# Index scores rectified in PSUM, half of the u projection dealt out between them, a fourth search tile on VectorE

## The chip, the cores and the metric

The kernel runs on one core of one Trainium2 chip. The metric is the device time of one execution, in microseconds; lower is better. TensorE multiplies into PSUM, VectorE (DVE) and ScalarE (ACT) read and write PSUM and SBUF, GpSimd (POOL) works on SBUF alone, and SyncE (SP) issues most of the DMAs. Each engine works through its own queue in order.

## What is computed

One layer of a hybrid decoder, for 1024 tokens of width 1024, in float32. The part that the change touches:

```python
h = rms_norm(x, norm1_g) * (1.0 + sc1) + sh1
proj = h @ w_in
u_ssm, q, k, v, q_idx, k_idx, w_idx = split(proj)
# S5 head group: diagonal state-space model of u_ssm
# sparse attention head group, per query t:
logits = relu(einsum('bthd,bsd->bths', q_idx, k_idx))          # 8 index heads of 64
score = einsum('bth,bths->bts', w_idx, logits) * IDX_SCALE
score = where(causal, score, -inf)
_, sel = top_k(score, 256)                                     # then attention over the selected keys
```

After that come group norms, one output projection and a squared-ReLU MLP; the change leaves them as they are.

## The kernel before

The 1024 queries are eight tiles of 128. Tiles 0 and 1 have at most 256 causal keys and need no selection; tiles 2 to 7 are the six search tiles, whose score rows are 384, 512, 640, 768, 896 and 1024 wide (`W` in `select`; search tile i is query tile i+2). Float32 products are made of three matmuls on split operands (`mm3`, L90 to L92: high·high, high·low, low·high), so every weight is loaded (`raw`), its high part taken by ScalarE (`wh`, L470) and its low part by GpSimd (`wl`, L472). There are two `raw` buffers and six of `wh` and `wl` each; a group of 256 columns of w_in takes four of the six, a group of 128 columns (the index queries) two.

The parts run as Python generators that `weave` advances by turns. What they issue goes to a scheduler which orders each engine's queue by priority (the order of issue) and by its own estimate of when operands are ready, so a later part can be placed ahead of an earlier one that waits. `later` issues a generator at a lower priority, and `tc.issue_after(ins)` puts the TensorE instructions of its block behind the one named in TensorE's queue.

The stages around the change, with the names of the code:

- `s5_setup` (VectorE, small operations) ends while the index stage has begun. `s5_tables` builds, for each of eight blocks, three tables on GpSimd (12 instructions a block) and stores each to HBM from SP's queue; the S5 scan loads them again much later (`s5_load_tables`, `s5_load_rot`).
- `index_proj`: for four groups of two index heads, `index_q` projects and splits the index queries and `index_score` makes the scores. For each search tile and head it makes two halves of the row in a two-bank PSUM tile (L551, L552), ScalarE writes relu(scale·score) for the whole row into an SBUF tile `r` (L556), and VectorE adds sign·r to the sum in SBUF (L558 for the first head, L560 for the seven others). After the eighth head L517 masks the diagonal block of each tile. The tables are advanced one step each round.
- `proj_qu`: u in two groups of 256 columns, eight tiles each, stored to HBM (L576, L577) and read back in another layout (L579); then q in two groups, with its norm's sums (L592, L593) and `rsqrt_q`.
- `select`: mean and variance of each search tile (L681 to L704), nine threshold passes over all six tiles (L707 to L724; `SEL_DVE` = 0, 1, 5 on VectorE, `SEL_ACT` = 4, 3, 2 on ScalarE), an exact end for each tile on VectorE (L734 to L741), a flag that says whether any row failed (a matmul with ones, L752, then L754, read into a VectorE register for a branch over the exact fallback), and then per tile the bias step that turns scores into 0 or -1e30 (L785 to L790).
- `attention` and `s5` are woven, then `glu`, `ada_rest`, the output projection and the MLP.

## Time and profile before

| | us |
|---|---|
| three runs, median (lowest to highest) | 1360.86 (1357.33 to 1362.24) |
| the profiled execution, its own time | 1360.31 |
| its span in the trace | 1358.5 |
| TensorE busy in the span | 1216.1 (90%) |
| VectorE busy | 1017.4 (75%) |
| ScalarE busy | 616.7 (45%) |
| GpSimd busy | 364.7 (27%) |

The span is the time from the first to the last instruction in the trace; 1.8 us of the execution's own time lie around it. The busy shares are averages over stages that have different limits, so the stage that is changed is read for itself. Matmuls overlap in their pipeline: a TensorE that is shown as wholly busy need not be at its peak, and the distance between the starts of two matmuls tells what one costs.

### The profile page before, as it was taken

The page shows a single profiled execution, that of the slowest core. Times are in us where ns is not written, and L with a number is a line of the kernel's source. Part 1 is how long each engine was busy: PE and PEld are TensorE (multiplying, and loading weights), DVE is VectorE, ACT ScalarE, POOL GpSimd, SP SyncE. Part 2 cuts the span into 40 slices and gives each one's busy share as a digit, 9 for nine tenths or more (in the row PEclk, how much of TensorE's full clock was granted, in tenths as well). Part 3 has the DMA queues.
Part 4 walks back from the last instruction along what each step waited for, and adds up shares of the span by engine and source line. Part 5 has one row for each costly group of instructions (what it writes and reads, how often), then busy time and mean ns, then how long its engine had stood idle before and what let it go on. Part 6 is the DMA issues. An engine that isn't in the chain of part 4 may idle for free.

```text
span 1358.5 us, 18554 instructions
## 1 busy us (share of the span) xinstructions
PE 1216.1 (90%) x6414; PEld 1038.1 (76%) x6414; DVE 1017.4 (75%) x1894; ACT 616.7 (45%) x1231; POOL 364.7 (27%) x350
## 2 busy tenths in 40 slices
PE   4987987935898999999979999999988999999997
PEld 4876887934788889888857788888866878788785
DVE  6599947897978763347795677677678888876887
ACT  6454453584777775724242333333224334333330
POOL 3072799861643453711100000000000000000125
PEclk9797989975899997999989999999998999999999
DMA  9511122350231572422412444433457735436252
GB/s 330 131 41 40 60 97 91 133 149 9 71 103 51 179 231 71 133 78 93 160 66 93 148 146 163 155 141 138 163 197 275 254 95 193 132 95 210 84 185 109
DMA packets 119327, 179.83 MB, mean 132 GB/s; under 512 B 28864, under 2 KB 63680, under 8 KB 119232
## 3 DMA queue, kind: packets, MB, share of 16 engines
q1 hardware_dynamic: 118160, 178.61, 40.1%
q8 instruction: 50, 0.82, 0.3%
q14 instruction: 45, 0.37, 0.1%
q10 hardware_dynamic: 1072, 0.03, 0.0%
HBM read 128.92 MB, written 48.50 MB: 131 GB/s over the span
## 4 chain that ended last, share of the span: by engine, by line
PE 51%; DVE 12%; DMA 4%; ACT 2%; issue 2%; POOL 2%; SPq 1%; DVEq 0%; ACTq 0%; POOLq 0%
PE pS L90 10%; PE pS L91 10%; PE pS L92 10%; PE pg L90 5%; PE pg L91 5%; PE pg L92 5%; DMA awa<-w_ada 2%; PE po L1274 2%; DVE fm L472 2%; PE pg L269 1%; PE pg L1258 1%; DVE acc L1871 1%; DVE acc L1845 1%; DVE fw L472 1%; POOL wol L472 1%
## 5 line engine op out<-in xcount | busy, mean ns | idle before, releaser
L1845 POOL TENSOR_TENSOR acc<-acc,g 128x512 f32<-128x512 f32 x4 | 5.9, 1499 | 579.1 <-DVE acc L1871 579.1
L91 PE MATMUL pg<-wl,hh 128*128 128x256 f32 (+1 forms) x288 | 81.6, 284 | 13.0 <-POOL wl L472 13.0
L470 ACT ACTIVATE fm<-ar 128x512 fp32r<-128x512 f32 x56 | 34.9, 624 | 119.9 <-PE pg L91 55.1
L90 PE MATMUL pg<-wh,hh 128*128 128x256 f32 (+1 forms) x288 | 81.0, 285 | 3.7 <-ACT wh L470 2.6
L1274 PEld LDWEIGHTS po<-v,pt 128*128 128x128 f32 x576 | 77.5, 208 | 6.0 <-ACT pt L1261 3.8
L1274 PE MATMUL po<-v,pt 128*128 128x64 f32 x576 | 78.8, 285 | 3.5 <-ACT pt L1261 3.3
L92 PE MATMUL pg<-wh,hl 128*128 128x256 f32 (+1 forms) x288 | 81.4, 284 | 0.0
L560 DVE SCALAR_TENSOR_TENSOR sc<-r,wsgn,sc 128x384 f32<-128x384 f32 (+5 forms) x42 | 56.0, 1344 | 28.5 <-ACT r L556 27.3
L90 PE MATMUL pS<-fm 128*128 128x512 f32 x160 | 62.2, 400 | 4.7 <-DVE z L1874 4.4
L91 PEld LDWEIGHTS pg<-wl,hh 128*128 128x128 f32 x288 | 55.1, 191 | 14.0 <-POOL wl L472 13.4
L91 PE MATMUL pS<-fm 128*128 128x512 f32 x160 | 63.1, 397 | 0.3 <-DVE fm L472 0.3
L92 PE MATMUL pS<-fm 128*128 128x512 f32 x160 | 62.9, 395 | 0.0
L1245 DVE CUSTOM_DVE_ANT_0 P<-pS,sc,rq 128x384 f32<-128x384 f32 (+5 forms) x48 | 43.9, 941 | 20.9 <-PE pS L1241 12.8
L90 PEld LDWEIGHTS pg<-wh,hh 128*128 128x128 f32 x288 | 54.3, 190 | 5.0 <-ACT wh L470 2.8
L556 ACT ACTIVATE r<-pS,wabs 128x384 f32<-128x384 f32 (+5 forms) x48 | 40.6, 848 | 36.4 <-PE pS L552 27.7
L92 PEld LDWEIGHTS pg<-wh,hl 128*128 128x128 f32 x288 | 54.9, 191 | 0.4
L470 ACT ACTIVATE fw<-ax 128x512 fp32r<-128x512 f32 x42 | 26.2, 623 | 61.1 <-PE pS L91 29.6
L1261 ACT ACTIVATE pt<-pg 128x512 f32<-128x512 f32 (+1 forms) x80 | 42.2, 547 | 22.2 <-PE pg L1258 21.8
L1258 PE MATMUL pg<-ident,P 128*128 128x128 f32 x288 | 49.2, 292 | 3.0 <-DVE zl L1340 1.3
L1247 ACT ACTIVATE P<-P,mx 128x128 f32<-128x128 f32 (+7 forms) x64 | 49.1, 769 | 5.7 <-DVE mx L1245 5.5
L90 PE MATMUL pS<-woh,mh 128*128 128x512 f32 x128 | 51.2, 400 | 0.0
L92 PE MATMUL pS<-woh,ml 128*128 128x512 f32 x128 | 50.9, 398 | 0.0
(606 smaller groups left out, 4154.1 us busy)
## 6 DMA issues: line engine op xcount, KB each, us to landing
awa<-w_ada SPq DMA_DIRECT2D x32, 512.0 KB, 4.3
a_d<-ws SPq DMA_DIRECT2D x64, 256.0 KB, 2.7
wr<-w_ff SPq DMA_DIRECT2D x32, 512.0 KB, 6.3
w1r<-w_ff SPq DMA_DIRECT2D x15, 1024.0 KB, 5.2
ax<-a_d SPq DMA_DIRECT2D x56, 256.0 KB, 2.8
ar<-a_d SPq DMA_DIRECT2D x56, 256.0 KB, 2.9
a_d<-c SPq DMA_DIRECT2D x45, 256.0 KB, 2.0
x<-x SPq DMA_DIRECT2D x16, 512.0 KB, 5.1
```

The source lines that it names most:

```text
L90: T.matmul(out, lh, rh, start=start, stop=False, **kw)
L91: T.matmul(out, lh, rl, start=False, stop=False, **kw)
L92: self.pe = T.matmul(out, ll, rh, start=False, stop=stop, **kw).ins
L470: nc.scalar.activation(hi, x, AF.Copy)
L472: e.tensor_tensor(lo, x, f(hi), op=OP.subtract)
L556: S.activation(rv, ps[:, :, :n], AF.Relu, scale=self.wabs[:, qt, h:h + 1])
L560: V.scalar_tensor_tensor(sc, rv, self.wsgn[:, qt, h:h + 1], sc, op0=OP.mult, op1=OP.add)
L1245: V.tensor_tensor_reduce(pv, ps[:, :nj, :m], bv, scale=self.rq[:, qt, h:h + 1], scalar=-NEG, op0=OP.add, op1=OP.min, accum_out=mx)
L1247: S.activation(p[:, :w], p[:, :w], AF.Exp, scale=-1.0, bias=mx, accum_out=LS[qt][:, h:h + 1])
L1258: T.transpose(ps[:, o:o + 128], P[n][h][:, (k0 + i) * 128:(k0 + i + 1) * 128], self.ident)
L1261: S.activation(pt[:, :m], ps[:, :m], AF.Copy)
L1274: T.matmul(po[:, o:o + HD], pt[:, (2 * i + h) * 128:(2 * i + h + 1) * 128], self.v[:, k0 + i, kv * HD:(kv + 1) * HD], start=(o == 0 and k0 ...
```

## The change

1. Scores. ScalarE's relu writes back into the PSUM tile it reads, half by half, and VectorE adds from PSUM. Rows of 384 and 512 take one bank of the four-buffer ring and one instruction of each; the four wider ones take two halves. The causal mask goes into the first head's pass for the last 128 columns, and L517 goes. The SBUF tiles `r` go (`knd` gets its own two).
2. u. The first group (`proj_u(0)`) is a generator of the index stage, one k-step (three matmuls) per round, and every u matmul is put behind the latest score matmul that has been issued. The second group is issued after the last score and is therefore behind all scores.
3. Tables. Of the eight blocks, the first four are issued in the index stage. Blocks 4 to 7 begin with a small copy on GpSimd that reads `self.gate`, so they wait: for `gs`, which the statistics of `select` make, or, for those issued after the flag, for `need`.
4. Search. Tile 2 (640 wide) moves from ScalarE to VectorE, and VectorE updates the threshold of each tile by two operations on one column instead of three on all of VectorE's columns (two before the loop).
5. Flag. A DMA turns `bad` into a row of one partition and a maximum makes the flag; the matmul goes.
6. Bias steps. They are advanced one for one with the first attention steps, with the S5 steps behind, where before they were issued ahead of both.

```diff
-SEL_DVE = (0, 1, 5)
-SEL_ACT = (4, 3, 2)
+SEL_DVE = (0, 1, 2, 5)
+SEL_ACT = (4, 3)
@@ build
-            self.index_proj(ix, tab)
+            self.index_proj(ix, itertools.islice(tab, 10 * TABG))      # TABG = 4
...
-            for i in range(2 * NT * 2):
+            for i in range(3 * NT):
                 next(qu)
-                next(tab, None)
-                if i % 2 or i >= 29:
+                if self.gate is not None and i < 21:
+                    next(tab, None)
+                if (i + 1) * 17 // (3 * NT) > i * 17 // (3 * NT):
                     self.weave([(sel, 1)], n=1)
             self.weave([(sel, 1)])
-            self.weave([(sel, 1)])
+            next(sel)
             self.weave([(tab, 1)])
...
-            self.weave([(s5, 1)], att, 2, n=2)
+            self.weave([(att, 1), (sel, 1)], s5, 1, until=sel)
             self.weave([(s5, 1)], att, 1)
@@ index_proj
+        u0 = self.proj_u(0)
         for c in range(4):
...
+            gens.append((itertools.islice(u0, 12 if c < 3 else 24), 1 if c < 3 else 2))
             self.weave(gens, tab, TABN)
-        for qt in range(2, 8):
-            dg = self.bias[qt][:, qt * 128:]
-            V.scalar_tensor_tensor(dg, dg, NEG, self.caus, op0=OP.max, op1=OP.min)
+        self.weave([(u0, 1)])
@@ index_score
+                    o = ps[:, j, :n]
+                    ks = slice(j * n, (j + 1) * n)
+                    T.matmul(o, lq, self.kih[:, ks], start=True, stop=False)
+                    self.last_sc = T.matmul(o, lq, self.kil[:, ks], start=False, stop=True).ins
+                    S.activation(o, o, AF.Relu, scale=self.wabs[:, qt, h:h + 1])
+                    sc, sg = self.bias[qt][:, ks], self.wsgn[:, qt, h:h + 1]
+                    if h:
+                        V.scalar_tensor_tensor(sc, o, sg, sc, op0=OP.mult, op1=OP.add)
+                        continue
+                    d = n - 128 if j == nj - 1 else n
+                    V.tensor_scalar(sc[:, :d], o[:, :d], sg, None, op0=OP.mult)
+                    if d < n:
+                        V.scalar_tensor_tensor(sc[:, d:], o[:, d:], sg, self.caus, op0=OP.mult, op1=OP.add)
@@ proj_u (new; proj_qu calls it for the second group)
+        wg = self.load_w([(C_U + c * 256, 256)], 256)
+        yield
+        for t in range(NT):
+            ps = self.bank()
+            tl = slice(t * 128, t * 128 + 128)
+            for k in range(KC):
+                wh, wl = wg[k]
+                with self.tc.issue_after(self.last_sc):
+                    self.mm3(ps[:, :256], self.hh[:, k, tl], self.hl[:, k, tl], wh, wl, k == 0, k == KC - 1)
+                if c == 0:
+                    yield
...
@@ select, in each of the eight passes
-            V.tensor_tensor(d, v[:, :NV], st1[:, k, :NV], op=OP.subtract)
-            V.scalar_tensor_tensor(t[:, :NV], c[:, :NV], float(TOPK), st2[:, k, :NV], op0=OP.is_ge, op1=OP.mult)
-            V.tensor_tensor(v[:, :NV], d, t[:, :NV], op=OP.add)
+                V.tensor_scalar(col(t, i), col(c, i), float(TOPK), st2[:, k, i:i + 1], op0=OP.is_ge, op1=OP.mult)
+                V.tensor_scalar(col(v, i), col(v, i), st1[:, k, i:i + 1], col(t, i), op0=OP.subtract, op1=OP.add)
@@ the flag
-        ps = self.bank()
-        T.matmul(ps[0:1, 0:1], bad, self.ones[:, 0:1], start=True, stop=True)
+        row = sp.tile([1, 128], F32, name="row")
+        nc.sync.dma_start(row, bad)
         fi = sp.tile([1, 1], I32, name="fi")
-        V.tensor_copy(fi, ps[0:1, 0:1])
+        V.tensor_reduce(fi, row, axis=AX.X, op=OP.max)
@@ s5_tables
+            if b >= TABG:
+                G.tensor_copy(cx[:, 0, 0:6], self.gate)
```

## Rows read from the trace of the kernel before

**Rows 1.** The page's first line.

```profile
span 1358.5 us, 18554 instructions
```

**Rows 2.** The table by stage: busy time, instructions, granted clock (PEclk).

```profile
core 0: us, PE busy (x) PEld busy (x) DVE busy (x) ACT busy (x) POOL busy (x), PEclk, DMA share, GB/s
...
174.00:206.00 32.00, 26.11 (x192) 25.32 (x191) 16.10 (x14) 14.72 (x24) 32.00 (x27) 0.89 0.31 101
206.00:242.00 36.00, 28.88 (x215) 27.99 (x214) 24.71 (x20) 13.60 (x21) 36.00 (x30) 0.91 0.29 93
242.00:257.00 15.00, 15.00 (x130) 15.00 (x129) 14.04 (x34) 2.75 (x7) 14.06 (x17) 1.00 0.61 204
257.00:297.00 40.00, 25.23 (x208) 24.41 (x207) 39.34 (x114) 39.59 (x116) 29.80 (x39) 0.91 0.31 94
297.00:318.00 21.00, 0.00 (x0) 0.02 (x1) 20.91 (x82) 3.06 (x10) 3.65 (x9) 0.50 0.34 97
...
330.00:460.00 130.00, 117.12 (x869) 106.85 (x869) 106.00 (x229) 100.85 (x218) 55.55 (x58) 0.94 0.28 78
```

**Rows 3.** TensorE's timeline, 194 to 240 us: start, duration, [idle before <- who ended it].

```profile
194.92 0.58 PE L91 MATMUL pg<-wl,hh 128*128 128x256 f32 x1 [5.89 <-POOL wl L472]
...
235.62 0.58 PE L91 MATMUL pg<-wl,hh 128*128 128x256 f32 x1 [7.12 <-POOL wl L472]
...
239.29 0.28 PE L92 MATMUL pg<-wh,hl 128*128 128x256 f32 x1
239.40 0.28 PE L90 MATMUL pg<-wh,hh 128*128 128x256 f32 x1
```

**Rows 4.** The timeline of GpSimd around 194 and 260 us.

```profile
193.61 2.49 POOL L472 TENSOR_TENSOR wl<-raw,wh 128x512 fp32r<-128x512 f32 x2
...
260.30 1.28 POOL L1046 TENSOR_TENSOR mt<-mt,mx 128x512 f32<-128x512 f32 x1
```

**Rows 5.** Groups by line and shape, VectorE, 100 to 260 us: busy, mean, idle.

```profile
L560 DVE SCALAR_TENSOR_TENSOR sc<-r,wsgn,sc 128x1024 f32<-128x1024 f32 x7 | 11.9, 1700 | 10.8 <-ACT r L556 10.6
...
L560 DVE SCALAR_TENSOR_TENSOR sc<-r,wsgn,sc 128x384 f32<-128x384 f32 x7 | 6.5, 924 | 0.2
```

**Rows 6.** The same view, ScalarE, 100 to 260 us.

```profile
L556 ACT ACTIVATE r<-pS,wabs 128x1024 f32<-128x1024 f32 x8 | 8.9, 1115 | 4.4 <-PE pS L552 4.4
...
L556 ACT ACTIVATE r<-pS,wabs 128x384 f32<-128x384 f32 x8 | 4.6, 581 | 4.3 <-PE pS L552 4.2
```

**Rows 7.** The same view, VectorE, 242 to 323 us.

```profile
L724 DVE TENSOR_TENSOR v<-d,t 128x3 f32<-128x3 f32 x8 | 3.8, 472 | 0.2
...
L738 DVE TENSOR_SCALAR ix<-cx 128x1 f32<-128x1 f32 x6 | 0.9, 149 | 0.0
```

**Rows 8.** The timeline of VectorE, single instructions of scoring, search and flag.

```profile
126.03 0.73 DVE L560 SCALAR_TENSOR_TENSOR sc<-r,wsgn,sc 128x512 f32<-128x512 f32 x1
...
260.21 0.16 DVE L712 SCALAR_TENSOR_TENSOR t<-c,gs 128x3 f32<-128x3 f32 x1
260.41 1.20 DVE L713 TENSOR_TENSOR v<-v,t 128x3 f32<-128x3 f32 x1
...
314.22 0.86 DVE L734 TENSOR_SCALAR_CACHE_REDUCE jv<-sc,hi 128x640 bf16<-128x640 f32 x1
...
318.23 0.15 DVE L754 CAST fi<-pg 1x1 int32<-1x1 f32 x1
...
322.13 0.19 DVE L620 TENSOR_SCALAR rq<-ry 128x48 f32<-128x48 f32 x1 [3.57 <-DVEq L759]
```

**Rows 9.** One line's view, L1159: min, median and max ns, first and last start.

```profile
L1159 DVE SCALAR_TENSOR_TENSOR y<-y,pg x8: 659/680/686, 364.5 to 443.3; 128x512 f32<-128x512 f32 x8
```

**Rows 10.** The timeline of TensorE at the flag.

```profile
318.01 0.19 PE L752 MATMUL pg<-ones,bad 128*1 128x1 f32 x2 [32.09 <-DVE rw L617]
```

**Rows 11.** One line's view, L577: issue to landing of a small store.

```profile
DMA to landing us min/median/max: 1.7/2.0/3.0
```

**Rows 12.** The timeline of SP's queue, the seventh load of an S5 table.

```profile
394.21 0.54 SPq L1074 DMA_DIRECT2D cl<-cl_d  x1
```

More of the change, by code (lines that the diff above doesn't have):

```diff
@@ L1 @@
+import itertools
 from contextlib import ExitStack
@@ L47 @@
 EARLY = 500
-LATER, TABN = 500, 1
+LATER, TABN, TABG = 500, 1, 4
 ON_V = [(k, 0) for k in (1, 2, 3, 5, 6)]
@@ L133, in build @@
             self.select_consts()
-            self.index_proj(ix, tab)
+            self.gate = None
+            self.u_d = self.dram.tile([L, DS], F32, name="u_d")
+            self.index_proj(ix, itertools.islice(tab, 10 * TABG))
             ix_close()
@@ L137, in build @@
             self.u = up.tile([128, 8, DS], F32, name="u")
-            self.u_d = self.dram.tile([L, DS], F32, name="u_d")
             qp, qp_close = self.pool("q", side="left")
@@ L440, in k_norm @@
         self.rstd(rk, self.kss[:, 4 * hf:4 * hf + 4].rearrange("p t h -> p (t h)"), HD, ix)
-        knd = ix.tile([128, NKV, 4, 2, HD], F32, name="knd", tag="r", bufs=3)
+        knd = ix.tile([128, NKV, 4, 2, HD], F32, name="knd", bufs=2)
         yield
@@ L543, in index_score @@
         for qt in range(2, 8):
-            n = (qt + 1) * 64
+            w = (qt + 1) * 128
+            nj = 1 if w <= 512 else 2
+            n = w // nj
             for i in range(2):
                 h = 2 * c + i
-                ps = self.bank2()
+                ps = self.bank()[:, None, :] if nj == 1 else self.bank2()
                 lq = qs[c][i][:, (qt - 2) * 128:(qt - 1) * 128]
-                for j in range(2):
+                for j in range(nj):
                     o = ps[:, j, :n]
-                    T.matmul(o, lq, self.kih[:, j * n:(j + 1) * n], start=True, stop=False)
-                    T.matmul(o, lq, self.kil[:, j * n:(j + 1) * n], start=False, stop=True)
-                sc = self.bias[qt].rearrange("p (j n) -> p j n", j=2)
-                r = ix.tile([128, L], F32, name="r", tag="r", bufs=3)
-                rv = r[:, :2 * n].rearrange("p (j n) -> p j n", j=2)
-                S.activation(rv, ps[:, :, :n], AF.Relu, scale=self.wabs[:, qt, h:h + 1])
-                if h == 0:
-                    V.tensor_scalar(sc, rv, self.wsgn[:, qt, h:h + 1], None, op0=OP.mult)
-                else:
-                    V.scalar_tensor_tensor(sc, rv, self.wsgn[:, qt, h:h + 1], sc, op0=OP.mult, op1=OP.add)
@@ new lines, in index_score, with proj_u @@
+                    d = n - 128 if j == nj - 1 else n
[3 more added lines that the diff above has]
+                yield
+    def proj_u(self, c):
+        nc = self.nc
+        wg = self.load_w([(C_U + c * 256, 256)], 256)
[8 more added lines that the diff above has]
+                if c == 0:
+                    yield
+            us = self.wp.tile([128, 256], F32, name="us", bufs=2)
+            nc.scalar.activation(us, ps[:, :256], AF.Copy)
+            nc.sync.dma_start(self.u_d[tl, c * 256:c * 256 + 256], us)
+            if c:
@@ L565, in proj_qu @@
         V, S, G, T = nc.vector, nc.scalar, nc.gpsimd, nc.tensor
+        u1 = self.proj_u(1)
+        next(u1)
         for c in range(2):
-            wg = self.load_w([(C_U + c * 256, 256)], 256)
             cs = slice(c * 256, c * 256 + 256)
-            for t in range(NT):
-                ps = self.bank()
-                tl = slice(t * 128, t * 128 + 128)
-                for k in range(KC):
-                    wh, wl = wg[k]
-                    self.mm3(ps[:, :256], self.hh[:, k, tl], self.hl[:, k, tl], wh, wl, k == 0, k == KC - 1)
-                us = self.wp.tile([128, 256], F32, name="us", bufs=2)
-                S.activation(us, ps[:, :256], AF.Copy)
-                nc.sync.dma_start(self.u_d[tl, cs], us)
-                yield
+            if c:
+                yield from u1
             nc.sync.dma_start(self.u[:, :, cs], self.u_d[:, cs].rearrange("(m j) n -> m j n", j=8))
@@ L700, in select @@
         V.tensor_tensor(gs, sd, self.slope, op=OP.mult)
+        self.gate = gs
         st1, st2 = (sp.tile([128, K, 6], F32, name=n) for n in ("st1", "st2"))
@@ L711, in select @@
             V.tensor_scalar(jv[:, :W[i]], B[i], col(v, i), None, op0=OP.is_ge, op1=OP.add, accum_out=col(c, i))
-        V.scalar_tensor_tensor(t[:, :NV], c[:, :NV], TOPK - 0.5, gs[:, :NV], op0=OP.subtract, op1=OP.mult)
-        V.tensor_tensor(v[:, :NV], v[:, :NV], t[:, :NV], op=OP.add)
+            V.tensor_scalar(col(t, i), col(c, i), TOPK - 0.5, col(gs, i), op0=OP.subtract, op1=OP.mult)
+            V.tensor_scalar(col(v, i), col(v, i), col(t, i), None, op0=OP.add)
         yield
@@ L750, in select @@
         yield "flag"
-        ps = self.bank()
-        T.matmul(ps[0:1, 0:1], bad, self.ones[:, 0:1], start=True, stop=True)
+        row = sp.tile([1, 128], F32, name="row")
+        nc.sync.dma_start(row, bad)
         fi = sp.tile([1, 1], I32, name="fi")
-        V.tensor_copy(fi, ps[0:1, 0:1])
+        V.tensor_reduce(fi, row, axis=AX.X, op=OP.max)
         X = st(6, "X", I32)
@@ L776, in select @@
             V.tensor_scalar(need, cx, -1.0, float(TOPK), op0=OP.mult, op1=OP.add)
+        self.gate = need
         yield
```

5 lines of the change are left out of this document (2 added, 3 removed).

## The prediction

> **What bounds the kernel now.** I read the table by stage first, because the shares of the whole span hide it, then the timelines of the engines that stand still in a stage, and last single operations for their prices. The edits lie in the stages from about 113 us (first scores) to 330 us (first attention steps); what comes behind has no edge to the wall clock, so I take it that it moves with them as a whole.
>
> From 146 to 242 us the index stage is TensorE's: VectorE is busy for only 16 of the 32 us from 174 to 206 [rows 2]. [...] In this stage the scheduler has put the whole u projection, though u is issued later. Twice TensorE stands still, 5.89 and 7.12 us, for `wl`, the low part of the next u or q weights [rows 3]. GpSimd makes it late because table instructions lie ahead of it: GpSimd is busy for all of 174 to 242 us, 27 instructions in 32 us or 1.2 us each [rows 2], and the `wl` came only at 193.61 [rows 4]. After each stop the matmuls run at half rate for a while (mean clock 0.89 and 0.91 in these stages, against 1.00 before and after) [rows 2]. The scores behind them in the queue wait too.
>
> From 257 to 318 us the search is VectorE's. It is busy for 39.3 of 40 and 20.9 of 21 us, while TensorE does 25.2 of 40 and nothing at all in the last 21 [rows 2]. ScalarE is full as well until 297 but falls idle then (3.1 of 21), and VectorE goes on alone. TensorE's 32.09 us of waiting end with the flag matmul at 318.01 [rows 10], which lies ahead of the first attention matmuls in its queue; VectorE passes the branch at 322.13 [rows 8]. So the change must be costed as two chains: when does the last score end (242 us now), and how long is it from there to the branch (80 us now).
>
> **Part 1, the index stage.** Half of u leaves it: 8 tiles x 8 k-steps x 3 = 192 matmuls x 0.117 = 22.5 us of a stage that TensorE bounds [rows 3]. They go behind the last score, into a stage where TensorE idles for 15 + 21 us [rows 2], so there they cost nothing; were that cover gone they would cost the 22.5 us again. The stops go as well, because no score waits any more for a group of weights that is loaded while the tables run: the second u group can't stand before a score, and the first group's weights and the index weights are all needed early. Each stop is worth its wait and the slow restart, 5.9 + 1.5 and 7.1 + 1.3 us, together 16 us (the restart: some 3 us at half rate).
>
> Against it: ScalarE now takes 80 instructions instead of 48. From 384 and 1024 columns (581 and 1115 ns [rows 6]) one costs 0.26 us + 0.83 ns a column, so the 32 extra ones cost at most 8.3 us over the stage, of an engine that is busy for 28 of the last 68 us [rows 2]: hidden. That the target is PSUM is shown nowhere here; I take the SBUF price, which with the fixed part halved or doubled is -10 to +21 us of ScalarE, still under its idle 40. VectorE takes 80 passes from PSUM, and 6 small ones for the mask. The same operation on 512 columns with one PSUM input is 680 ns (L1159 [rows 9]); with both inputs in SBUF it was 0.73 us at a moment when GpSimd was idle [rows 8], but over this stage the means are 924 ns for 384 columns and 1700 for 1024 [rows 5], 1.2 to 1.7 times that rate. The PSUM form keeps to 659 to 686 ns [rows 9] in a stage where GpSimd is 43% busy (55.6 of 130 us [rows 2]). 8 heads x (0.5 + 0.7 + 2 x (0.5 + 0.55 + 0.6 + 0.7) us) = 47 us, against 56 for L560 (six shapes, 7 instructions of each, 6.5 to 11.9 us [rows 5]). VectorE is relieved, and off this path but for the first head group, where `s5_setup` still holds it; so the relief counts nothing. [...]
>
> Pinning u behind each score takes TensorE's freedom to run ahead while a score waits for a PSUM buffer. A two-bank tile is now held until VectorE has read it, not until ScalarE has. For the widest row: matmuls 0.9, two relus of 0.69, two adds of 0.68 partly overlapped, some 3 us, with two tiles 1.5 us a score; 8 wide ones per head group need 12 us, below the 20 us of TensorE work in a group. I charge 4 us for imperfect turns; the bounds are 0 and 16.
> Sum: -22.5 - 16 + 4 = **-34.5 us**; the last score ends near 207 us (range -22 to -42).
>
> **Part 2, from the last score to the branch.** The statistics (242 to 257) hold small VectorE operations that wait for GpSimd: L713 ran for 1.20 us and ended with GpSimd's instruction [rows 4, 8], where its neighbour took 0.16. With blocks 4 to 7 held until `gs`, only weight splits are left beside the statistics: -4 us of 15 (0 to -7). Tile 2 on VectorE: nine passes of 0.86 us [rows 8] = +7.8 us, and VectorE is the bound here, so all of it counts. ScalarE's relief counts nothing: it was already done first. The updates: 3 operations on 24 become 8 on one column each. The old ones are 26 operations of three columns, between 0.16 us (L712 [rows 8]) and 472 ns (the mean of L724 [rows 7], again from waiting): 4 to 12 us, half way 8. The new form is like L738, one column, 149 ns, never longer while GpSimd worked [rows 7]. 72 of them at 0.06 us (fill between passes) to 0.20 (dependent neighbours, 260.21 to 260.41 [rows 8]) are 4.3 to 14.4; I take 0.11, as the scheduler can put them behind another tile's pass: 8, so 0 net (-8 to +10). The flag by DMA: `bad` to 318.23 was 0.5 us with the matmul; a small store lands in 1.7 to 3.0 us [rows 11], with issue and reduction +2.5. The rest of the q work stays in VectorE's queue a little longer: +1. Sum: **+7.3 us** (-5 to +20). TensorE has 22.5 us of u and 45 of q in 87 us: done before the branch.
>
> **Part 3, the start of attention.** TensorE's queue no longer holds the flag matmul, so the first transposes and scores can precede the branch: -2 us (0 to -5). The bias steps were already mixed with the first attention steps by the scheduler, so their new order is worth nothing on its own. Blocks 6 and 7 are issued after the flag with gate `need`: 24 GpSimd instructions x 1.2 = 29 us in that same stage, where VectorE is 82% busy [rows 2]. Their tables are first wanted some 70 us behind the branch (394.21 against 322.13 [rows 8, 12]), so they are in time; but they make VectorE wait and stand ahead of S5's own GpSimd steps: +3 (0 to +10). Queues passed: SP gets one more DMA (the row) among table stores; POOL four small copies.
>
> Sum: -34.5 + 7.3 - 2 + 3 = -26.2 us. Against the profiled execution (1360.3 us of its own; span 1358.5 [rows 1]) that is **1334 us**; the median of the runs, 1360.9, is the same within 0.6.
>
> **Rivals.**
> (a) The stops move but stay. GpSimd still has 48 table instructions and the second u group's weights behind them; if TensorE waits for `wl` among the scores as now, 16 us are not won: 1350 us. For it: GpSimd is full in that stage. Against it: no weights are due there.
> (b) The search stretches. VectorE's queue is in order, and a q reduction that stands among the passes waits if TensorE is late with q (two changes of weight groups, 5 to 7 us each as in [rows 3]); or the updates cost 0.20: +12 us, 1346 us.
> (c) The gain is larger. If statistics and updates lose all their waiting and the turns cost nothing: -42 - 2 - 3 = 1313 us.
> (d) Slower. The tables of blocks 6 and 7 sit ahead of S5's steps in GpSimd's queue and hold the scan back for their whole 29 us, and up to 38 where VectorE blocks them; as the scan's end starts the next stage, this decides from 26 us on: 1334 + 38 = 1372 us. Against it: 70 us of slack in the loads, and 74 idle GpSimd us.
> (e) The change doesn't do what it says: the PSUM ring holds TensorE up (16 us instead of 4) and u's weights come late as well, so that the stage ends hardly earlier: 1358 us.
>
> **How the numbers follow.** Forecast 1334: 47%. (a) 14%, (b) 12%, (c) 15%, (d) 7%, (e) 5%. A measurement here tells some 0.5% (7 us) from no change. Faster by more: the forecast, (b), (c) and most of (a), 83%; within: (e) and the rest of (a) and (d), 10%; slower: (d), 7%. The range 1313 to 1354 leaves out (d), (e) and the edges of (a) and (c), some 18%.
>
> **What would show it.** Right: no u matmul of the second group before the last score; that score's last add near 207 us; no TensorE wait for `wl` above 2 us among the scores; L560's successor near 0.7 us for 512 columns; passes of the search at 4.5 to 5 us a round, full VectorE; the branch near 295 us. Wrong: scores that wait for a PSUM tile in every turn, VectorE idle within the search, or S5's first steps waiting for table instructions on GpSimd.

## The result, and the profile after

The change makes the kernel slower: six runs of it have a median of 1383.75 us (1377.07 to 1385.81), six of the kernel before 1361.93 us; the ratio is 1.0149, with a 95% interval of 1.0127 to 1.0172. The prediction was 1334 us. The profiled execution took 1377.07 us, with a span of 1375.3; its span is 16.8 us longer than that of [rows 1].

The page's first line, and the table by stage over the stretches of [rows 2], of the changed kernel:

```profile
span 1375.3 us, 18643 instructions
...
core 0: us, PE busy (x) PEld busy (x) DVE busy (x) ACT busy (x) POOL busy (x), PEclk, DMA share, GB/s
174.00:206.00 32.00, 26.99 (x134) 20.79 (x133) 21.64 (x36) 20.57 (x38) 24.00 (x27) 1.00 0.22 72
206.00:242.00 36.00, 32.80 (x242) 29.95 (x243) 30.83 (x86) 20.23 (x44) 19.36 (x22) 1.00 0.35 109
242.00:257.00 15.00, 14.84 (x126) 14.63 (x125) 15.00 (x55) 14.81 (x42) 14.28 (x16) 1.00 0.36 123
257.00:297.00 40.00, 39.36 (x335) 39.12 (x333) 32.95 (x115) 16.26 (x44) 19.42 (x27) 1.00 0.21 61
297.00:318.00 21.00, 0.00 (x0) 0.00 (x0) 16.39 (x55) 0.61 (x1) 8.78 (x10) 0.54 0.23 71
330.00:460.00 130.00, 107.19 (x801) 97.29 (x801) 96.02 (x221) 92.60 (x209) 58.78 (x66) 0.87 0.27 72
```

TensorE is now busy through the search (39.4 of 40 us from 257 to 297 against 25.2), as the change wants it. But behind it stands a hole. VectorE's timeline around the flag, then TensorE's, ScalarE's, GpSimd's and SP's from there (line numbers are those of the changed kernel: L804 to L809 are the bias step, L1043 to L1082 the tables, L1245 the copy of qT, L1261 the attention scores):

```profile
304.44 0.15 DVE L767 TENSOR_REDUCE bad<-ok 128x1 f32<-128x6 f32 x1
...
306.60 0.28 DVE L772 TENSOR_REDUCE fi<-row 1x1 int32<-1x128 f32 x1 [0.68 <-DMA row<-bad]
...
310.61 0.20 DVE L630 TENSOR_SCALAR ry<-rq 128x48 int32<-128x48 int32 x1 [3.66 <-DVEq L777]
...
344.80 0.47 PE L1261 MATMUL pS<-kTh,qT 128*128 128x128 f32 x1 [48.44 <-ACT qT L1245]
...
311.95 0.61 ACT L804 ACTIVATE ja<-sc,ntau 128x384 bf16<-128x384 f32 x1 [16.05 <-DVE ntau L798]
...
340.85 1.04 ACT L804 ACTIVATE ja<-sc,ntau 128x896 bf16<-128x896 f32 x1 [6.03 <-DVE eq L808]
344.15 1.08 ACT L1245 ACTIVATE qT<-pg 128x512 fp32r<-128x512 f32 x2 [2.26 <-DMA pt_d<-pt]
...
310.59 0.19 POOL L1043 COPY cx<-need 128x6 f32<-128x6 f32 x1 [8.72 <-DVEq L777]
...
342.04 0.32 SPq L1082 DMA_DIRECT2D pt_d<-pt  x1
```

VectorE passes the branch at 310.61 us, 11.5 us earlier than at 322.13 in [rows 8]. Yet TensorE, which has ended the last projection and the first transposes at 296.4, waits 48.44 us and starts its first attention scores at 344.80, where the kernel before has them at 321.45:

```profile
321.45 0.46 PE L1240 MATMUL pS<-kTh,qT 128*128 128x128 f32 x1
```

What it waits for is the copy of qT on ScalarE. That copy was released at 344.15, 2.1 us behind the issue of the last table store (342.04): a DMA that has nothing to do with q. In the built program qT lies at bytes 108544 to 116736 of each partition and the table buffers at 106976 to 116192; the attention pool is opened on the memory that the tables' pool gives back. The Sign operations of the first five bias steps stand ahead of qT in ScalarE's queue as well, 6 to 10 us apart. The fifth ends at 341.9, so in this order of the queue the store alone adds the last 2.3 us (the 2.26 in qT's row); why the queue has this order is a question for experiment 6.

The way from the first difference to the end, from the two timelines (us; a minus is earlier than before):

| step | forecast | measured | from |
|---|---|---|---|
| last score | -34.5 | -16.2 | 242.5 to 226.3 |
| to the first search pass | -4 | -8.5 | 14.7 to 6.2 long |
| passes and exact ends, to `bad` | +8.8 | +11.5 | 60.5 to 71.9 |
| `bad` to the branch | +2.5 | +1.7 | 4.4 to 6.2 |
| branch to the first attention scores | -2 | +34.9 | -0.7 to 34.2 |
| from there to the end of the span | +3 | -6.5 | 1037.0 to 1030.5 |

Against the forecast the profiled execution is 43.1 us long: 18.3 of it arise in the first row, -2.6 in the next three and 27.4 in the last two.

The index stage, in two views. First, what TensorE waited for from 113 to 227 us (in total, times, longest); second, TensorE's busy time and clock in the stages that end with the last score, the flag, the first copy of zh (the glu stage, behind S5) and the end of attention, of before and of the changed kernel (after the busy time: matmuls, clock, DMA share, GB/s):

```profile
PE pS L556 <- DVE sc L561: 13.6, 18, 3.6
PE pS L556 <- DVE sc L564: 2.2, 1, 2.2
PE pg L91 <- DVE sc L566: 2.0, 1, 2.0
```

```profile
113.00:242.50 129.50, 114.61 (x784) 0.94 0.24 77
242.50:318.00 75.50, 39.73 (x332) 0.81 0.38 115
318.00:451.00 133.00, 118.12 (x867) 0.90 0.26 73
451.00:575.00 124.00, 118.22 (x763) 0.91 0.48 151
```

```profile
113.00:226.50 113.50, 94.47 (x497) 0.90 0.16 52
226.50:304.50 78.00, 69.70 (x591) 0.96 0.33 102
304.50:465.00 160.50, 112.19 (x841) 0.82 0.32 91
465.00:592.00 127.00, 122.63 (x778) 0.89 0.44 138
```

Both stops for `wl` of [rows 3] are gone. In their place TensorE waits 18.7 us in all, 23 times, for VectorE to add a score and free its PSUM tile (three smaller groups are not shown). 10.5 us of these waits lie before 170 us, beside the S5 setup, and 8.2 behind it, where VectorE itself waits for ScalarE's relu (VectorE's own waits from 170 to 227 us):

```profile
DVE sc L561 <- ACT pS L558: 14.6, 19, 5.0
```

Busy time multiplied by the window's mean clock gives 107.7 us of full-speed work before and 85.0 after, 22.7 less; idle time rises from 14.9 to 19.0 us; and what is lost to the low clock rises from 6.9 to 9.4. Together -16. The split into work and lost time is an estimate, because the mean clock counts idle time too (it is 0.54 from 297 to 318 us of the changed kernel, where TensorE does nothing).

### The profile page after: what moved, and what is told of

Read it like the earlier page. It is cut to its first block, busy times and chain, and to the rows that moved or that the text cites. A ratio compares the mean times of both kernels' runs of the same rounds, so it can differ in the third digit from the quotient of the medians.

```text
span 1375.3 us, 18643 instructions
## 1 busy us (share of the span) xinstructions
PE 1222.3 (89%) x6380; PEld 1035.4 (75%) x6380; DVE 1020.7 (74%) x1989; ACT 609.7 (44%) x1227; POOL 340.6 (25%) x354
## 4 chain that ended last, share of the span: by engine, by line
PE 54%; DVE 10%; DMA 4%; POOL 3%; ACT 2%; issue 2%; SPq 2%; DVEq 0%; ACTq 0%; POOLq 0%
PE pS L91 10%; PE pS L92 10%; PE pS L93 10%; PE pg L91 5%; PE pg L92 5%; PE pg L93 5%; PE po L1295 3%; DVE fm L474 2%; PE pg L1279 2%; PE pg L271 1%; SPq L1125 1%; DMA awa<-w_ada 1%; DMA woraw<-w_out 1%; DVE acc L1892 1%; PE pS L1261 1%
## 5 line engine op out<-in xcount | busy, mean ns | idle before, releaser
L472 ACT ACTIVATE fm<-ar 128x512 fp32r<-128x512 f32 x56 | 34.9, 624 | 119.6 <-PE pg L92 54.6
L1261 PE MATMUL pS<-kTh,qT 128*128 128x384 f32 (+5 forms) x96 | 39.4, 413 | 50.5 <-ACT qT L1245 48.4
L1261 PEld LDWEIGHTS pS<-kTh,qT 128*128 128x128 f32 x96 | 20.3, 211 | 52.6 <-ACT qT L1245 48.7
L474 POOL TENSOR_TENSOR wl<-raw,wh 128x512 fp32r<-128x512 f32 (+1 forms) x28 | 34.2, 1234 | 72.0 <-ACT wh L472 72.0
```

Of the source, the lines that this page charges most:

```text
L472: nc.scalar.activation(hi, x, AF.Copy)
L474: e.tensor_tensor(lo, x, f(hi), op=OP.subtract)
L1261: T.matmul(ps[:, j, :m], QT[qt][:, h, :], self.kTh[kv][:, sl], start=True, stop=False)
```

## Experiments

Each is compared with runs of the kernel before on the same chip. Different experiments ran on different chips, on which the kernel before took 1360.0 to 1362.0 us, so a difference between two of them is also given by their ratios. `ntau` is the first step behind the branch on VectorE (322.5 us in the kernel before, 311.8 in the changed one).

| | kernel | median us | ratio to before (95%) | `ntau` us |
|---|---|---|---|---|
| 1 | changed, tables ahead of the flag | 1365.2 | 1.0032 (1.0010 to 1.0053) | 320.8 |
| 2 | 1, GpSimd load later | 1383.3 | 1.0164 (1.0120 to 1.0208) | 321.5 |
| 3 | before, two blocks late | 1379.7 | 1.0133 (1.0090 to 1.0177) | 318.0 |
| 4 | 1, six blocks ungated | 1361.4 | 1.0008 (0.9985 to 1.0032) | 315.8 |
| 5 | 4, bias order of before | 1360.5 | 0.9999 (0.9976 to 1.0022) | 317.2 |
| 6 | 4, GpSimd load in place | 1384.9 | 1.0156 (1.0105 to 1.0208) | 316.7 |
| 7 | 4, relu to SBUF | 1370.7 | 1.0071 (1.0045 to 1.0097) | 322.2 |
| 8 | 4, no pins | 1371.1 | 1.0082 (1.0056 to 1.0107) | 334.0 |
| 9 | 5, three search tiles | 1358.8 | 0.9976 (0.9956 to 0.9996) | 311.0 |
| 10 | 5, last setup chain left out | 1357.4 | 0.9970 (0.9943 to 0.9996) | 306.5 |
| 11 | 5, flag by matmul | 1366.5 | 1.0036 (1.0011 to 1.0060) | 313.1 |
| 12 | before with parts 1 and 2 alone | 1360.4 | 0.9998 (0.9976 to 1.0021) | 308.6 |
| 13 | 9, own buffer for a table | 1362.3 | 0.9999 (0.9976 to 1.0022) | 312.7 |
| 14 | 12, own buffer for a table | 1355.9 | 0.9961 (0.9947 to 0.9975) | 308.7 |
| 15 | before, ten passes more | 1368.0 | 1.0038 (1.0024 to 1.0052) | 337.6 |
| 16 | 12, ten passes more | 1365.4 | 1.0027 (1.0008 to 1.0046) | 321.0 |
| 17 | 14, q ahead of u | 1369.0 | 1.0055 (1.0037 to 1.0073) | 324.7 |
| 18 | 14 again | 1355.6 | 0.9950 (0.9935 to 0.9965) | 311.0 |

### 1 and 4: all tables ahead of the flag

```diff
-                if self.gate is not None and i < 21:
-                    next(tab, None)
+                if self.gate is not None:
+                    for _ in range(2):
+                        next(tab, None)
# experiment 4 besides:
-LATER, TABN, TABG = 500, 1, 4
+LATER, TABN, TABG = 500, 1, 6
```

> The changed kernel with two table steps instead of one in each turn of the search, so that all eight blocks are built before the flag and none waits for `need`. Theory M (memory: the attention's first tiles lie in the bytes of the table buffers, so TensorE's first attention scores cannot come before the last table store, 342 us in the changed kernel): first attention scores near 312 to 318 instead of 344.8, total 20 to 30 us below the changed kernel, 1354 to 1364. Rival Q (queues: the first attention steps stand in ScalarE's queue behind the bias steps, which GpSimd's table work slows): the same, since the table work is gone from that stage too. Rival O (order: it is the mixing of bias and attention steps itself that costs): no change, near 1383.

> As e1, but blocks 4 and 5 are issued in the index stage without a gate, so that GpSimd has half as much table work in the search. If GpSimd is crowded in the search of e1 (q norms and weight splits late), 3 to 8 us below e1; if not, within 3 us of it. If table work in the index stage holds the scores up, 3 or more above.

1365.2 and 1361.4 us: 18.6 and 22.3 us below the changed kernel (16 and 19 by the ratios), so the two late blocks cost it 16 to 22 us, and O, the order, does not. Experiment 1's first scores ran at 306 us, ahead of the flag, but its branch came 9 us later than the changed kernel's: its table work pushed q's norms (the last reduction at 312.2 instead of 301.1), and with them VectorE's search (`bad` at 312.9 instead of 304.4), back. Experiment 4 gets half of that again. But with the late tables gone, the change is no more than equal to the kernel before, though the branch is passed 6.7 us earlier.

### 3: the late tables alone, added to the kernel before

```diff
-            self.index_proj(ix, tab)
+            tab1 = itertools.islice(tab, 10 * TABG)      # TABG = 6
+            self.index_proj(ix, tab1)
...
-                next(tab, None)
+                next(tab1, None)
...
+        self.gate = need
...
+            if b >= TABG:
+                G.tensor_copy(cx[:, 0, 0:6], self.gate)
```

> The kernel before with one thing added: the tables of blocks 6 and 7 are issued after the flag and wait for `need`. M: attention cannot start before the last table store, some 30 us behind the branch at 322; with part given back later, 20 to 30 us slower than the kernel before, 1381 to 1391. Q: here qT stands ahead of the bias steps, so only contention is left, 2 to 8 us, 1363 to 1369.

19.7 us slower than the kernel before (interval 12 to 24), at the near end of what M expected and far from Q's 2 to 8. But Q's premise did not hold in the run: the scheduler put qT behind all six bias steps here too. So the run shows what late tables cost, and not by which of the two ways. ScalarE's last Sign and its qT, then TensorE's first scores, where the kernel before has 321.45:

```profile
348.63 1.15 ACT L790 ACTIVATE ja<-sc,ntau 128x1024 bf16<-128x1024 f32 x1 [6.00 <-DVE eq L794]
352.45 1.09 ACT L1231 ACTIVATE qT<-pg 128x512 fp32r<-128x512 f32 x2 [2.68 <-DMA pt_d<-pt]
...
353.10 0.47 PE L1247 MATMUL pS<-kTh,qT 128*128 128x128 f32 x1 [37.65 <-ACT qT L1231]
```

### 2 and 6: the same load on GpSimd, without the shared memory

```diff
# abridged from experiment 6; experiment 2 has two scratch tiles, in a pool of their own
+            self.weave([(self.later(self.dummy(sp), LATER), 1)])   # 6: where the late tables stand, scratch in a pool of select
+    def dummy(self, sp):
+        x = sp.tile([128, 576], F32, name="dmx")
+        for b in range(2):
+            G.tensor_copy(x[:, 0:6], self.gate)
+            for n, k in ((576, 3), (512, 3), (256, 6)):
+                for i in range(k):
+                    G.tensor_tensor(x[:, :n], kTh0[:, :n], kTh1[:, :n], op=OP.mult)
```

> As e1, plus a load on GpSimd in the place of the late tables: the same count and sizes of two-input instructions (24 and four small copies that wait for `need`), reading keys and writing scratch that shares no bytes with the attention's first tiles. Output unchanged. M: like e1, at most 6 us more from contention; first attention scores before 325. Q: like the changed kernel, within 6 us of 1383.

> Experiment 4 plus the GpSimd load of experiment 2 (24 two-input instructions and the copies that wait for `need`), but issued where the late tables of the changed kernel stand, and writing to a scratch tile that shares no bytes with tables or attention. Output unchanged. Theory M (shared memory holds the attention's start): first attention scores that go on running by 325 us, though GpSimd is full from 316 to 348. Q (bias steps slowed by GpSimd hold the attention's first steps in ScalarE's queue): TensorE idle until 345 or later, as in the changed kernel. Total: M 1365 to 1374 (contention and GpSimd's queue ahead of S5 remain, 18 us at most as in experiment 2), Q 1380 or more.

Attention's start goes as M says; the total doesn't. Experiment 2's load was placed by the scheduler behind 339 us, so it tells nothing of the start, but it costs 18 us there. In experiment 6 it begins at 316. With no shared bytes the scheduler puts the first qT copies ahead of the flag and of every bias step, the first scores run at 304.55, and TensorE goes on behind the branch beside the load. ScalarE's first qT, TensorE's scores, GpSimd's group of the load, and the stretch from 316 to 400 us of experiment 6 and of experiment 4:

```profile
303.91 1.07 ACT L1258 ACTIVATE qT<-pg 128x512 fp32r<-128x512 f32 x2
...
304.55 0.33 PE L1274 MATMUL pS<-kTh,qT 128*128 128x128 f32 x1 [0.70 <-ACT qT L1258]
...
318.22 0.47 PE L1274 MATMUL pS<-kTh,qT 128*128 128x128 f32 x1 [9.77 <-DVE mx L1279]
```

```profile
L1094 POOL TENSOR_TENSOR dmx<-kTh,kTh 128x256 f32<-128x256 f32 (+2 forms) x24 | 27.5, 1144 | 0.8
```

```profile
316.00:400.00 84.00, 60.70 (x353) 51.85 (x354) 72.78 (x154) 45.92 (x111) 55.98 (x61) 0.72 0.28 76
```

```profile
316.00:400.00 84.00, 71.52 (x475) 62.05 (x475) 68.88 (x182) 58.64 (x138) 37.10 (x44) 0.86 0.36 95
```

So the shared bytes are what keeps the first scores until 344.80 in the changed kernel, both through the order of ScalarE's queue and through the store at its end. But without them 27.5 us of GpSimd work, drawn out to 392 us between S5's own steps, cost as much: 1384.9 against 1361.4 (20 us by the ratios). In 84 us TensorE does 353 matmuls instead of 475, at a clock of 0.72 instead of 0.86, and S5's eight blocks take 97.5 us from the first to the last copy of kk, the product with which a block begins (333.4 to 430.9), instead of 80.8. In the changed kernel attention and S5 start later and S5 then runs faster (73.4 us), which ends at the same point, 431.5. M and Q were both wrong as alternatives: the late work costs some 20 us whether or not it also holds the start. What the shared bytes would cost without the GpSimd work was not run. Whether S5 waits in GpSimd's queue or through a slowed VectorE was not separated.

### 5: the order of the bias steps

```diff
-            next(sel)
+            self.weave([(sel, 1)])
             self.weave([(tab, 1)])
...
-            self.weave([(att, 1), (sel, 1)], s5, 1, until=sel)
+            self.weave([(s5, 1)], att, 2, n=2)
```

> Experiment 4 (six blocks ungated, all tables before the flag; branch at 315.9 us, 6.3 before the kernel before, yet the total only equal to it, 1361.4) with the order of the bias steps put back: all bias steps issued ahead of S5 and attention, and two attention steps in each of the first two S5 turns. Theory O (the new order lets S5 end with more attention left over: from the first zh copy to the last PV matmul experiment 4 needs 125.2 us, the kernel before 120.4): 4 to 8 us faster than experiment 4, 1353 to 1357, and that stretch back at about 120. Rival (the order is worth nothing on its own, as I had predicted): within 2 us of 1361.

The stretch went from 125.2 to 121.1 us in the profile, as O has it, but the medians differ by 0.9 us only, with intervals that overlap almost wholly. No effect that can be told: the rival, and the prediction's "worth nothing on its own", stand.

### 7, 8 and 10: what holds the index stage

```diff
# experiment 7: relu to SBUF (rr: three buffers, shared with knd)
-                    S.activation(o, o, AF.Relu, scale=self.wabs[:, qt, h:h + 1])
+                    S.activation(rr[:, ks], o, AF.Relu, scale=self.wabs[:, qt, h:h + 1])
+                    o = rr[:, ks]
# experiment 8: no pins
-                with self.tc.issue_after(self.last_sc):
-                    self.mm3(...)
+                self.mm3(...)
# experiment 10: powers of e2 left out
-        yield from cpow(self.e2c, self.e2s, 15)
+        V.memset(self.e2c[:, :, 2:], 0.0)
+        V.memset(self.e2s[:, :, 2:], 0.0)
```

> Experiment 4 with the relu written to an SBUF tile again, half by half, everything else as there. Theory P (a PSUM tile is held until VectorE has added it, and VectorE is late in the first half of the stage because of the S5 setup): TensorE's waits for VectorE's add among the scores, 18 us, go; last add 6 to 15 us earlier than 226, between 211 and 220; the total follows by as much, down to 1350, if the tables on GpSimd don't slow the SBUF adds. Rival (the scores are slowed by GpSimd contention on SBUF adds, which the PSUM form avoids): last add at 226 or later, total 1361 or more.

> Experiment 4 without the pins that put each u matmul behind the latest score. If the pins keep TensorE from filling its waits for PSUM with u: the waits inside the stage shrink and the last add comes 5 to 10 us earlier. If the scheduler then moves u ahead of scores: last add later or the same. I expect within 4 us of experiment 4.

> Experiment 5 without the last chain of the S5 setup on VectorE (the powers of e2, which lie among the scores from 143 to 164 us); they are set to zero by two instructions, so the S5 part of the output is not computed. Theory P (scores wait because VectorE, in order, frees their PSUM tiles only behind the setup): TensorE's waits for the adds before 165 us go, 3.6 + 2.6 us with the slow clock behind them; last add 5 to 10 us earlier than 226, total 1351 to 1356. Rival (the PSUM turns are slow whatever VectorE does): last add within 3 us of 226, total within 3 us of 1360.

Experiment 7: theory P fails as a remedy, and the rival's numbers come. The last add ends at 230.4 us, 3.7 later than in experiment 4, and the total is 9 us worse. The waits for VectorE are replaced by waits for ScalarE, VectorE is hardly idle between its adds (0.8 us ahead of those of 512 columns, 6.6 in the changed kernel), and the adds from SBUF take 1.5 times as long. Experiment 7's waits and its 512-column add, and the same add of the changed kernel:

```profile
PE pS L558 <- ACT r L560: 15.1, 16, 2.5
```

```profile
L564 DVE SCALAR_TENSOR_TENSOR sc<-r,wsgn,sc 128x512 f32<-128x512 f32 x21 | 23.5, 1124 | 0.8
```

```profile
L561 DVE SCALAR_TENSOR_TENSOR sc<-pS,wsgn,sc 128x512 f32<-128x512 f32 x14 | 10.4, 746 | 6.6 <-ACT pS L558 6.4
```

1124 ns against 746. In the kernel before the SBUF form of 512 columns has a mean of 1112 ns from 113 to 242.5 us, where GpSimd is busy for 100.1 of 129.5 us; with GpSimd idle it took 0.73 us [rows 8]. Whether GpSimd's work is what makes it dearer, and by which way, was not tested.

Experiment 8: without pins TensorE waits less (9.1 us for adds instead of 13.6), but the scheduler runs the second half of u and part of q ahead of scores, and the last add ends at 249.9 us. The pins are worth 10 us, where I had expected at most 4.

Experiment 10: without the chain the long waits go (longest 1.3 us instead of 3.6), yet the last add comes at 223.9, 2.9 us earlier, just inside the rival's 3 us, and the total is 3.1 us lower (4 by the ratios), though the step behind the branch comes 10.7 us earlier. Most of TensorE's waits stay:

```profile
PE pS L557 <- DVE sc L562: 7.5, 16, 1.3
PE pS L557 <- DVE sc L565: 4.1, 2, 2.2
```

So the setup on VectorE explains 3 us. The 8.2 us behind 170 us lie where VectorE waits for relu, so there the chain of matmul, relu and add in two tiles is long by itself; what the waits that are left in the first half hang on was not tested.

### 9 and 11: the search and the flag

```diff
# experiment 9
-SEL_DVE = (0, 1, 2, 5)
-SEL_ACT = (4, 3)
+SEL_DVE = (0, 1, 5)
+SEL_ACT = (4, 3, 2)
# experiment 11
-        nc.sync.dma_start(row, bad)
-        V.tensor_reduce(fi, row, axis=AX.X, op=OP.max)
+        T.matmul(ps[0:1, 0:1], bad, self.ones[:, 0:1], start=True, stop=True)
+        V.tensor_copy(fi, ps[0:1, 0:1])
```

> Experiment 5 (all tables before the flag, bias steps in the order of before; branch at 317 us, total 1360.5) with tile 2 of the search on ScalarE again: three tiles on VectorE, three on ScalarE; the one-column updates stay. Tile 2 costs VectorE nine passes of 0.87 us and nine updates of about 0.31, 10.6 us. Theory V (VectorE bounds the search): branch 7 to 11 us earlier, total 1350 to 1354. Rival (three tiles keep ScalarE for 4.4 us a round, as long as four keep VectorE, so that nothing is won): within 3 us of experiment 5.

> Experiment 5 with the flag by matmul again. From bad to the branch the DMA form took 7.1 us in experiments 4 and 5 (308.7 to 315.9), the matmul form 4.4 in the kernel before: 2 to 3 us earlier. But the matmul stands ahead of the first attention transposes and scores in TensorE's queue, which experiment 5 runs before the flag. I expect 1357 to 1361; above 1362 would show that the early attention steps are worth more than the DMA.

Experiment 9: `bad` comes 8.5 us earlier (301.5 against 310.0) and the step behind the branch 6.1, so VectorE does bound the search and the fourth tile is a loss there; but the total gains 1.7 us of it (3 by the ratios), not the 6 to 10 that V expected. Experiment 11: the branch is 4 us earlier and the total 6 us later (5 by the ratios). The flag matmul waits 6.2 us in TensorE's queue, ahead of the early attention steps.

### 12, 13 and 14: the index stage alone, and S5's loads

Experiment 12 is the kernel before with parts 1 and 2 of the change (search tiles, updates, flag, bias order and ungated tables as before). Experiments 13 and 14 add to 9 and 12:

```diff
-        mt = (big if b % 2 else ahead)("mt", tag=f"mt{b % 2}")
+        mt = (big if b else ahead)("mt", tag=f"mt{(b + 1) % 2 + 1}" if b else "mt0")
```

> The kernel before with parts 1 and 2 of the change alone (scores rectified in PSUM, the mask in the first head's pass, half of u dealt out between them); tables without gates, three search tiles on each engine, the old updates, the matmul flag and the old order of the bias steps. If the index stage's gain (last add at 226 instead of 242) reaches the end: 10 to 16 us below the kernel before, 1345 to 1351. If q, which now comes later, holds VectorE in the search, or the table work pushes q back: 1355 to 1362.

> Experiment 9 with a buffer of its own for block 2's mt table, so that its load no longer waits for block 0's transposes at the head of SP's queue (there: mt at 322.7, the rot loads of blocks 0 and 1 only behind it, where the kernel before loaded them at 291 to 303). Theory L (late table loads hold S5 and with it the end): rot loads from about 303 us, first zh copy 5 to 10 us earlier than 444, total 5 to 10 us below experiment 9, 1349 to 1354. Rival T (from the branch on TensorE's own idle and slow stretches bound the stage, whatever S5 does): loads early, total within 3 us of 1359.

> Experiment 12 with the same extra buffer. L: rot loads from 304 instead of 322 us, total 5 to 10 us below experiment 12, 1350 to 1355. T: within 3 us of 1360.

Experiment 12 passes the branch 13.9 us earlier than the kernel before and ends where it does. In the traces the lead melts on the way: it is 13.7 us at the first product of attention weights and values (317.95 against 331.62), 7.8 at the last copy of kk, 6.0 at the first of zh, and nothing at the end of attention (572.3 against 571.9). Its SP queue shows one reason to look at: the load of block 2's mt table, which waits for block 0, stands at the head of the queue, and S5's first rotation tables only behind it, at 322 us, where the kernel before had loaded them by 303. They go into bytes of the projection operands, which are read until 303 now that half of u runs in the search. SP's queue of experiment 12, and of experiment 14:

```profile
322.02 0.33 SPq L1096 DMA_DIRECT2D mt<-mt_d  x1
322.39 2.47 SPq L1104 DMA_DIRECT2D rot<-pt_d  x4
```

```profile
306.25 2.66 SPq L1104 DMA_DIRECT2D rot<-pt_d  x4
```

The loads come early in both repaired kernels. Experiment 14 gains 4.5 us on 12 (5 by the ratios), and as experiment 18 it has the same time again; experiment 13 gains nothing on 9, and S5's first block starts no earlier in either (328.3 and 325.8 us). So late loads are not what pins the end; that they cost 4.5 us in one of two cases is all that can be said.

### 15 and 16: does the end follow the branch?

```diff
+        for _ in range(10):
+            V.tensor_scalar(jv[:, :W[NV - 1]], B[NV - 1], col(tau, NV - 1), None, op0=OP.is_ge, op1=OP.add, accum_out=col(c, 0))
         need, ok = st(6, "need"), st(6, "ok")
```

> The kernel before with ten more passes over the widest score row on VectorE ahead of the flag, 10 x 1.35 us, results unused: branch at 335.6 instead of 322.1. If the stages behind move as a whole: total 1371 to 1376. If S5 or attention have slack there: less, down to 1362.

> Experiment 12 with the same ten passes: branch back at about 322 us, where the kernel before has it. If the end is pinned by something other than the branch (late loads, L): 1360 to 1363, as experiment 12. If the end follows the branch and experiment 12 lost its lead through something unrelated to it: 1370 to 1375.

The edit is not the delay that the expectations speak of. The scheduler put three of the ten passes ahead of `bad` and seven behind it, between the flag and the branch and, in experiment 15, among the first steps of attention. Experiment 15's first scores, its first product with the values, and `ntau`:

```profile
326.95 0.42 PE L1242 MATMUL pS<-kTh,qT 128*128 128x128 f32 x1
...
334.33 0.95 PE L1276 MATMUL po<-v,pt 128*128 128x64 f32 x4
...
337.64 0.17 DVE L781 TENSOR_SCALAR ntau<-tau 128x6 f32<-128x6 f32 x1 [2.46 <-DVEq L761]
```

`ntau` and with it the bias steps come 15.1 us later than in the kernel before, but the first scores only 5.5 and the first product with the values 2.7. The median rises by 0.38% (0.24 to 0.52), some 5 us. The profiled execution is the slowest of its seven, and its span is 13.3 us longer than that of the kernel before. In experiment 16 `ntau` comes 12.4 us later than in experiment 12, the first scores 7.4, the first product 9.6, and the median 5.0, with an interval from nothing to 8 us by the ratios. So a later branch costs something in both, less than its shift in the medians; what share of a shift reaches the end these two runs can't tell.

### 17 and 18: q ahead of u, and the best version again

Experiment 17 moves the second group of u behind both groups of q in `proj_qu`; experiment 18 is experiment 14 with more rounds.

> Experiment 14 with q projected ahead of the second half of u in the search. The q norms (16 reductions and the rsqrt chains on VectorE) come 22 us earlier, u's second half later. If late q norms on VectorE hold search or attention: branch 1 to 4 us earlier than 308.7 and total 3 to 8 us below experiment 14, 1348 to 1353. If not, or if u comes too late for S5's first blocks: within 3 us of 1356, or above.

> Experiment 14 again with more rounds. If its 0.9961 was no chance: a ratio to the kernel before between 0.994 and 0.998, the interval below 1.

Experiment 17 is 13 us slower than 14: the search takes longer, not shorter (`bad` at 312.4 us instead of 303.0), the branch comes 16 us later and S5's first block 10.8. Moving q ahead is no remedy; whether late q norms held experiment 14 it can't show, because the search itself grew by 9.4 us. Experiment 18 settles that 12 with the extra buffer is faster than both kernels, if by little: 0.9950 of the kernel before, some 7 us.

## Why the prediction was wrong

**Part 3 failed, and carries the result.** The step was "their tables are first wanted some 70 us behind the branch, so they are in time; ... +3 (0 to +10)". From the branch to the end of the span +1 was forecast and +28.4 came; the two late blocks cost 20 us added to the kernel before (experiment 3) and 16 to 22 of the changed kernel's (experiments 1 and 4). I costed the late tables by when their results are read, and GpSimd by its busy share. I did not ask what the tables' buffers become when the work is done: the attention's first tiles. So TensorE starts its first scores 34 us behind the branch. Nor would the rest have been +3: GpSimd work beside S5, with no shared bytes, costs 20 to 23 us in experiment 6. Rival (d), that work ahead of S5's steps, had 7%; its price is inside its 38, but whether the wait is in GpSimd's queue, as it says, stays open. Its argument against, idle GpSimd time, was a mean over a stage.

**Part 1: the terms were right but one.** -34.5 was forecast and -16.2 came, outside its range. Half of u left as priced (22.7 us of full-speed work against 22.5; in the kernel before twelve matmuls of 256 columns in a row start within 239.05 to 240.33 us, 0.116 us apart at a clock of 1.00), and both stops went (13.0 us), so rival (a) is out. The charge for "imperfect turns", 4 us with 16 as its upper bound, measured 18.7, and the slow clock did not give back 3 us but, by that estimate, cost 2.5 more. I had compared the turn of a wide tile (some 3 us, two tiles) with TensorE's work as a sum over a head group; the waits come turn by turn. The S5 setup on VectorE explains 3 us of them (experiment 10), and behind it TensorE waits 8.2 us though VectorE itself waits for relu. This is the first half of rival (e), a little above its 16 us; its second half, late weights of u, did not come. (The range's far end of -42 is more than its terms give: with turns at nothing they sum to -38.5, and (c) to some 1317.) "So the relief counts nothing" missed the reverse: an engine off the path came onto it, because it now frees the buffers.

**Part 2: the sum was right, its terms were not.** +7.3 was forecast and +4.7 came. The stretch to the first pass won 8.5 us instead of 4: 4.0 because all but 0.9 of the 4.9 us of bn statistics now run between the last scores, and 4.6 because the small operations behind them take 5.3 us instead of 9.9, with only weight splits on GpSimd beside them. The passes and ends cost 11.5 instead of 8.8. The two one-column updates take 0.31 us a tile (rows of 0.21 and 0.27 us, 0.12 and 0.19 from start to start), where I had 0.22, and once VectorE waits 6.95 us for a q norm, as rival (b) has it:

```profile
238.12 0.27 DVE L742 TENSOR_SCALAR v<-v,st,t 128x1 f32<-128x1 f32 x1
238.31 0.21 DVE L741 TENSOR_SCALAR t<-c,st 128x1 f32<-128x1 f32 x1
238.43 0.87 DVE L740 TENSOR_SCALAR_CACHE_REDUCE jv<-sc,v 128x640 bf16<-128x640 f32 x1
...
266.46 0.42 DVE L611 TENSOR_REDUCE rq<-qsq 128x4 f32<-128x256 f32 x1 [6.95 <-POOL qsq L610]
```

**The premise under all three failed too.** "What comes behind has no edge to the wall clock, so I take it that it moves with them as a whole": in experiments 9, 10 and 12 the branch comes 11 to 16 us earlier than in the kernel before, and 0 to 4 us of it are gained at the end; in 14 and 18 it comes 12 to 14 us earlier, and 5 to 7 are gained. Which resource takes the rest was not settled. From `bad` to the end of attention TensorE's idle time is 19.7 us in the kernel before and 24 to 31 in experiments 5, 9, 10, 12 and 14. The largest growth is in its waits for VectorE's first attention steps, 4.0 us before and 10.4 and 11.6 in 12 and 9; the rest is spread, and S5's loads are not it.

Of the signs that the prediction named, "scores that wait for a PSUM tile" showed, if not in every turn, and VectorE idle within the search once (6.95 us). "S5's first steps waiting for table instructions" named the right work, but in the changed kernel S5's first matmuls stand behind the attention steps, which wait for the tables' memory.

## What to carry to other kernels

Before work is moved later, look up what its buffers become: this kernel stacks its pools, so the late store (issued at 342.04 us) held qT, which is opened on that memory next, until 344.15, and nothing in the trace of before shows it, because there the last table store is issued at 287.33 and the first scores run at 321.45. When a second engine is put between a PSUM tile and its release, price the turn with what else is in that engine's queue: here the waits came to 18.7 us instead of 4. And test with a delay how much of a stage's gain reaches the end before a gain at its start is counted whole, and look in the trace where the scheduler has put the delay: here seven tenths of it landed behind the point that it was meant to hold.

## What the runs showed that I had not expected

Beside GpSimd's table work VectorE's bias steps take up to three times as long. The steps of the 512-wide tile in the changed kernel, beside table work:

```profile
323.65 2.06 DVE L806 TENSOR_TENSOR_SCAN pre<-eq 128x512 f16<-128x512 bf16 x1
325.74 1.07 DVE L807 TENSOR_SCALAR eq<-pre,need 128x512 bf16<-128x512 f16 x1
```

In the kernel before, with GpSimd idle, the same two take 1.23 and 0.35 us, while the eight search passes of 640 columns (L740 above) take 0.87 to 0.89 us, beside table work as without it. And ScalarE's relu is not dearer with its target in PSUM: 660 ns for 512 columns, where 689 ns was its mean into SBUF.
